# Both attention heads' scores side by side in three PSUM banks, five banks for the rest, and the row sums transposed first in a round

## The chip, the cores and the metric

The kernel runs on one core of one Trainium2 chip. The engines are named as the profile names them: PE (TensorE, the matrix multiplier, with PEld for its weight loads), DVE (VectorE), ACT (ScalarE), POOL (GpSimd) and SP (SyncE, which issues the transfers). PE writes its results to PSUM, a memory of eight banks of 512 fp32 values in each of 128 partitions; DVE and ACT read them there. The metric is the device time of one execution in microseconds (us), as the median of several runs.

## The reference, cut to what matters

Two transformer layers over 512 latent tokens and 256 context tokens (768 in all), 1024 features, everything in fp32. Layer 0 mixes tokens with grouped-query attention (16 query heads, 4 key heads), layer 1 with latent attention (16 heads). Latent queries attend to all 768 keys; in layer 0 the context queries attend to the 256 context keys.

```python
def block_attention(q, k, v):
    def one_block(qi):                                   # 128 queries
        s = jnp.einsum('bqhgd,bkhd->bhgqk', qi, k) * scale
        p = jax.nn.softmax(s, axis=-1)
        return jnp.einsum('bhgqk,bkhe->bqhge', p, v)
...
for i in range(DEPTH):                                   # 2 layers
    y_lat, y_ctx = gqa_mixer(...) if i == 0 else mla_mixer(...)
    x = layer_norm(alpha * x + g_a * y_lat, ...)
    x = layer_norm(alpha * x + g_m * sq_relu_mlp(x * (1 + sc_m) + sh_m, w1, w2), ...)
    # layer 0 does the same for the context tokens
```

## The kernel before

The program runs through its stages once: the modulation vectors and layer 0's projections (to about 129 us), the first attention (to about 340 us), its output projection, layer 0's MLP, layer 1's projections, the second attention (1074 to about 1265 us), its output projection and layer 1's MLP. The products run as fp32r matmuls on operands that are split into a high and a low part (names ending in h and l, or H and L).

Both attentions are `Attn.run` (L752), with 8 pairs of heads. The work is cut into rounds. A full round is one block of 128 queries for both heads of a pair; there are four per pair in each attention, 64 in all. The first attention has one more round per pair for the 256 context queries, 8 in all. The order of PE's instructions within the attentions is that of the code (`manual_schedule`, L785); the order on the other engines is set by a scheduler. In each pass of the loop PE does, in this order:

1. the scores of this round, first head, then second head (`score`, L766, with L848 in layer 0, L840 for context queries, L1351 in layer 1). A head's 768 scores per query lie in a tile `big` of two banks, 384 in each. There are two such tiles, one per head and round, so a tile comes back in the next round.
2. the transposes of the round before (`turn`, L776): 12 per full round (L707), into three tiles `one` of one bank each, which ACT (L710) and DVE (L712) copy to SBUF as `pT`.
3. the end of a finished product with the values, where there is one (`end`, L736): two transposes of the reciprocal row sums (L740) into the bank that holds the product, a copy by ACT (L742) and a multiply by DVE (L743).
4. a preparation step of the next pair, where there is one (L800): transposes of queries (L610, L1307) or a key projection (L89 to L91), through a `one`.
5. half of the product of an earlier pair of rounds with the values (L731), into a `one` that stays taken until its `end`.

Behind each head's scores, DVE finds the row maximum (L690, result `nm`) and ACT the exponentials and their sums (L691, an ACTIVATE followed by a read of the accumulator, result `prob`). In a context round these are L693 and two activations of L695. There are four tiles `one`; two `big` tiles of two banks and four `one` make up the eight banks. During the first attention POOL and the DMA queues work on modulation vectors of later stages, and PE, ACT and DVE have small instructions of that work and of the query preparation among those of the rounds.

A tile that is to be overwritten makes the writer wait until the readers of what is in it have finished. The wait stands in the program as a count of finished instructions on the reader's engine.

Of the kernel before, what the change touches and what calls it, by code (L numbers as in the profile page):

```python
# [11 lines left out]
F32 = mybir.dt.float32  # L12
F32R = mybir.dt.float32r
AF = mybir.ActivationFunctionType
# [25 lines left out]
def backbone(ctx, tc, a, out):  # L40
# [9 lines left out]
    const = pool(ctx, "const")  # L50
    wpool = pool(ctx, "wpool")
    dram = pool(ctx, "dram", space=DRAM)
    ps = pool(ctx, "ps", space=PSUM)

    def big():
        return ps.tile([P, 2, 512], F32, name="big", tag="big", bufs=2)

    def one():
        return ps.tile([P, 512], F32, name="one", tag="one", bufs=4)

    def split_hi(dst, src):
        return nc.scalar.copy(out=dst, in_=src)  # L62
# [610 lines left out]
    class Attn:  # L673
# [6 lines left out]

        def softmax(self, S, ntile, width, sm):


            ap = self.ap
            nm = ap.tile([P, 2], F32, name="nm", tag="nm", bufs=3)
            pt = ap.tile([P, 768], F32, name="prob", tag="prob", bufs=4)
            pv = pt[:, 0 : 2 * width].rearrange("p (b w) -> p b w", b=2)
            sv = S[:, :, 0:width]
            if ntile == 1:
                nc.vector.tensor_reduce(out=nm[:, 0:1], in_=sv, axis=AX.XY, op=ALU.max, negate=True)  # L690
                nc.scalar.activation(pv, sv, AF.Exp, bias=nm[:, 0:1], accum_out=sm)  # L691
            else:
                nc.vector.tensor_reduce(out=nm, in_=sv, axis=AX.X, op=ALU.max, negate=True)  # L693
                for i in range(2):
                    nc.scalar.activation(  # L695
                        pv[:, i], sv[:, i], AF.Exp, bias=nm[:, i : i + 1], accum_out=sm[:, i : i + 1]
                    )
            return pt
# [53 lines left out]
        def run(self, first, prep, scores, vcol, o_of, npair, ctx_scores, fill, at):  # L752

            rounds = []
            for p in range(npair):
                rounds += [(p, 0, 0)] + ([(p, None, 0)] if ctx_scores is not None else [])  # L760
                rounds += [(p, 0, 1), (p, 1, 0), (p, 1, 1)]
            state, PT, sums = {0: first}, {}, {}
            av, steps, ends, last = [], [], [], []
            n = 0

            def score(p, hf, q, h):  # L766
                S = big()
                if (p, hf) not in sums:
                    sums[p, hf] = self.ap.tile([P, 2, 2], F32, name="sm", tag="sm", bufs=4)
                if hf is None:  # L770
                    ctx_scores(state[p], h, S)
                    return self.softmax(S, 2, CTX, sums[p, hf][:, :, h])
                scores(state[p], h, NCT + hf * 2 + q, S)
                return self.softmax(S, 1, 384, sums[p, hf][:, q, h : h + 1])

            def turn(p, hf, q, pts):  # L776
                if hf is None:
                    PT[p, hf] = t = self.ap.tile([P, 2, NCT, 2, P], F32, name="pC", tag="pC")
                    self.transposed(pts, t.rearrange("p t n h c -> p (t n) h c"), 1)
                    return  # L780
                if q == 0:
                    PT[p, hf] = self.ap.tile([P, 2, NT, 2, P], F32, name="pT", tag="pT", bufs=2)
                self.transposed(pts, PT[p, hf][:, q], self.nact)

            with tc.manual_schedule(engines={nc.tensor.engine}):  # L785
                while rounds or last or av or ends:
                    now = []
                    if rounds:
                        p, hf, q = rounds.pop(0)
                        if hf == 0 and q == 0 and p + 1 < npair:  # L790
                            state[p + 1], steps = prep(p + 1)
                        now = [(p, hf, q, [score(p, hf, q, h) for h in range(2)])]
                    ready, ended = av[:1], ends
                    ends = []
                    for it in last:
                        turn(*it)
                    for f in ended:
                        f()
                    if steps:
                        steps.pop(0)()  # L800
                    for f, end in ready:
                        f()
                        ends += [end] if end else []
                    av = av[1:]
                    if last and (last[0][1] is None or last[0][2] == 1):
                        p, hf = last[0][:2]
                        lo = 0 if hf is None else NCT + hf * 2
                        av += self.values(
                            PT[p, hf], sums[p, hf],
                            lambda kt, hh, p=p: vcol(kt, 2 * p + hh), range(NCT if hf is None else NT),  # L810
                            o_of(p)[:, lo : lo + 2, :],
                        )
                    last = now
                    for i in (n, n + 1):
                        if fill is not None:
                            fill(i % 5 < 2)
                        for f in at.get(i, []):
                            f()
                    n += 2
                if fill is not None:  # L820
                    fill.rest()

    st_x.close()
    st_att = ExitStack()
# [15 lines left out]
    def ctx_scores0(st, h, S):  # L840
        pr, QS = st
        kv = pr // 2
        for i in range(2):
            lhsT = QS[h][:, i * P : (i + 1) * P]
            nc.tensor.matmul(S[:, i, 0:CTX], lhsT, KL[:, kv, 0:CTX], start=True, stop=False)
            nc.tensor.matmul(S[:, i, 0:CTX], lhsT, KH[:, kv, 0:CTX], start=False, stop=True)

    def scores0(st, h, qt, S):  # L848
        pr, QS = st
        kv = pr // 2  # L850
        lhsT = QS[h][:, qt * P : (qt + 1) * P]
        for c in range(2):
            cs = slice(c * 384, c * 384 + 384)
            nc.tensor.matmul(S[:, c, 0:384], lhsT, KL[:, kv, cs], start=True, stop=False)
            nc.tensor.matmul(S[:, c, 0:384], lhsT, KH[:, kv, cs], start=False, stop=True)

    phase[0] = "pool"
    ada_ts, ada_bias4 = [], vec_bias(0, 4, 0, 1)
# [492 lines left out]
    def scores1(st, h, qt, S):  # L1351
        kh, kl, QH, QL = st
        cols = slice((qt - NCT) * P, (qt - NCT + 1) * P)
        for c in range(2):
            cs = slice(c * 384, c * 384 + 384)
            nc.tensor.matmul(S[:, c, 0:384], QL[:, h, cols], kh[:, h, cs], start=True, stop=False)
        for c in range(2):
            cs = slice(c * 384, c * 384 + 384)
            nc.tensor.matmul(S[:, c, 0:384], QH[:, h, cols], kl[:, h, cs], start=False, stop=False)
            nc.tensor.matmul(S[:, c, 0:384], QH[:, h, cols], kh[:, h, cs], start=False, stop=True)  # L1360

    o1 = {}

# [141 lines left out]
```

## Time and profile before

| | |
|---|---|
| median of 3 runs | 1697.6 us (1696.79 to 1701.78) |
| the profiled execution's own time | 1703.23 us |
| its span, first to last instruction | 1701.4 us |
| PE busy | 1629.9 us (96% of the span) |
| DVE, ACT, POOL busy | 1111.5, 719.5, 450.6 us |
| mean granted TensorE clock | 0.989 of full speed |

The span is the time from the first to the last recorded instruction; the execution's own time is 1.83 us more. Busy times add up the instructions of an engine; PE's matmuls overlap, so that a row's duration is longer than the step from one matmul to the next. An idle time is named by what ended it. The granted clock is 1.00 at full speed and 0.50 at the lower of TensorE's two levels (2.4 and 1.2 GHz).

### The profile page before, as it was taken

The page shows a single profiled execution, that of the slowest core. Times are in us where ns is not written, and L with a number is a line of the kernel's source. Part 1 is how long each engine was busy: PE and PEld are TensorE (multiplying, and loading weights), DVE is VectorE, ACT ScalarE, POOL GpSimd, SP SyncE. Part 2 cuts the span into 40 slices and gives each one's busy share as a digit, 9 for nine tenths or more (in the row PEclk, how much of TensorE's full clock was granted, in tenths as well). Part 3 has the DMA queues.
Part 4 walks back from the last instruction along what each step waited for, and adds up shares of the span by engine and source line. Part 5 has one row for each costly group of instructions (what it writes and reads, how often), then busy time and mean ns, then how long its engine had stood idle before and what let it go on. Part 6 is the DMA issues. An engine that isn't in the chain of part 4 may idle for free.

```text
span 1701.4 us, 23714 instructions
## 1 busy us (share of the span) xinstructions
PE 1629.9 (96%) x9266; PEld 1369.1 (80%) x9266; DVE 1111.5 (65%) x1700; ACT 719.5 (42%) x1317; POOL 450.6 (26%) x317
## 2 busy tenths in 40 slices
PE   8997998999999999999999899999999999999996
PEld 6775776778888888898889798888778888888884
DVE  4778778755756666556447776766658655555577
ACT  3324666644633344333122356666663532222221
POOL 0247889000323345224003431000004200000034
PEclk9998999999999999999999999999999999999998
DMA  8312113033434356344212232001013533322322
GB/s 323 133 66 90 51 57 100 26 136 112 161 122 138 112 184 198 114 147 146 68 50 85 73 104 90 1 1 38 21 60 122 182 99 99 99 98 88 99 75 75
DMA packets 51969, 172.05 MB, mean 101 GB/s; under 512 B 6776, under 2 KB 6928, under 8 KB 51856
## 3 DMA queue, kind: packets, MB, share of 16 engines
q1 hardware_dynamic: 51824, 170.51, 29.8%
q8 instruction: 73, 1.20, 0.3%
q14 instruction: 40, 0.33, 0.1%
q10 hardware_dynamic: 32, 0.02, 0.0%
HBM read 161.03 MB, written 9.47 MB: 100 GB/s over the span
## 4 chain that ended last, share of the span: by engine, by line
PE 68%; DVE 12%; DMA 7%; POOL 6%; ACT 4%; issue 2%; SPq 0%; DVEq 0%; POOLq 0%; ACTq 0%
PE one L89 9%; PE one L91 9%; PE one L90 9%; PE big L977 7%; PE big L981 6%; PE big L980 6%; DMA araw<-in_w_ada_dram 4%; PE one L731 4%; PE one L917 2%; PE one L921 2%; PE one L918 2%; DVE wl L65 2%; PE one L707 2%; POOL aacc L208 2%; DMA raw<-in_mlp_w_dram 2%
## 5 line engine op out<-in xcount | busy, mean ns | idle before, releaser
L62 ACT CAST wh<-raw 128x1024 fp32r<-128x1024 f32 (+3 forms) x172 | 171.9, 1016 | 399.3 <-PE one L91 213.2
L65 DVE TENSOR_TENSOR wl<-raw,wh 128x1024 fp32r<-128x1024 f32 (+3 forms) x172 | 219.8, 1291 | 173.1 <-ACT wh L62 171.6
L977 PE MATMUL big<-actH,wh 128*128 128x384 f32 (+2 forms) x800 | 280.4, 351 | 1.6 <-ACT wh L62 1.6
L981 PE MATMUL big<-actH,wl 128*128 128x384 f32 (+2 forms) x800 | 279.7, 350 | 0.8 <-DVE wl L65 0.8
L980 PE MATMUL big<-actL,wh 128*128 128x384 f32 (+2 forms) x800 | 279.6, 350 | 0.0
L89 PE MATMUL one<-wh,hh 128*128 128x512 f32 x640 | 256.3, 402 | 12.6 <-ACT hh L62 7.0
L91 PE MATMUL one<-wh,hl 128*128 128x512 f32 x640 | 254.5, 399 | 5.3 <-DVE hl L65 5.3
L90 PE MATMUL one<-wl,hh 128*128 128x512 f32 x640 | 255.5, 399 | 1.3 <-DVE wl L65 1.3
L1059 DVE TENSOR_TENSOR yacc<-yacc,one 128x512 f32<-128x512 f32 x260 | 174.0, 682 | 109.9 <-PE one L91 109.6
L208 POOL TENSOR_TENSOR xr<-xr,raw 128x1024 f32<-128x1024 f32 x49 | 129.7, 2647 | 244.8 <-ACT raw L206 229.6
L977 PEld LDWEIGHTS big<-actH,wh 128*128 128x128 f32 x800 | 150.1, 188 | 15.0 <-ACT wh L62 2.4
L981 PEld LDWEIGHTS big<-actH,wl 128*128 128x128 f32 x800 | 150.1, 188 | 14.1 <-DVE wl L65 1.4
L980 PEld LDWEIGHTS big<-actL,wh 128*128 128x128 f32 x800 | 150.2, 188 | 12.3 <-issue 0.4
L89 PEld LDWEIGHTS one<-wh,hh 128*128 128x128 f32 x640 | 122.0, 191 | 44.5 <-ACT hh L62 8.0
L691 ACT ACTIVATE prob<-big,nm 128x768 f32<-128x768 f32 x128 | 116.2, 908 | 92.2 <-DVE nm L690 91.8
L91 PEld LDWEIGHTS one<-wh,hl 128*128 128x128 f32 x640 | 121.5, 190 | 35.0 <-DVE hl L65 6.2
L90 PEld LDWEIGHTS one<-wl,hh 128*128 128x128 f32 x640 | 122.1, 191 | 27.5 <-DVE wl L65 1.7
L328 POOL TENSOR_TENSOR xr<-xr,ln_g 128x1024 f32<-128x1024 f32 x14 | 37.2, 2658 | 390.9 <-DMA xr<-xres 384.6
L690 DVE TENSOR_REDUCE nm<-big 128x1 f32<-128x768 f32 x128 | 119.8, 954 | 31.8 <-PE big L1360 19.0
L707 PE MATMUL one<-ident,prob 128*128 128x128 f32 x832 | 104.8, 275 | 2.9 <-ACT pT L710 2.0
L731 PE MATMUL one<-pT,V 128*64 128x256 f32 x768 | 98.0, 391 | 5.7 <-DVE pT L712 4.5
L707 PEld LDWEIGHTS one<-ident,prob 128*128 128x128 f32 x832 | 96.0, 142 | 6.8 <-ACT pT L710 2.7
(245 smaller groups left out, 2822.9 us busy)
## 6 DMA issues: line engine op xcount, KB each, us to landing
raw<-in_mlp_w_dram SPq DMA_DIRECT2D x128, 512.0 KB
raw<-in_w_ada_dram SPq DMA_DIRECT2D x56, 512.0 KB
sraw<-in_w_ada_dram SPq DMA_DIRECT2D x16, 512.0 KB
araw<-in_w_ada_dram SPq DMA_DIRECT2D x32, 256.0 KB
raw<-in_w_o_dram SPq DMA_DIRECT2D x16, 512.0 KB
xr<-xres SPq DMA_DIRECT2D x14, 512.0 KB
raw<-in_w_qkv_dram SPq DMA_DIRECT2D x12, 512.0 KB
xres<-z SPq DMA_DIRECT2D x10, 512.0 KB
```

The lines of the kernel that those rows point to most:

```text
L62: return nc.scalar.copy(out=dst, in_=src)
L65: return nc.vector.tensor_tensor(out=dst, in0=src, in1=hi.bitcast(F32), op=ALU.subtract)
L89: nc.tensor.matmul(o, lh, rh, start=start, stop=False)
L90: nc.tensor.matmul(o, lh, rl, start=False, stop=False)
L91: nc.tensor.matmul(o, ll, rh, start=False, stop=stop)
L208: nc.gpsimd.tensor_tensor(out=accs[s], in0=accs[s], in1=dst, op=ALU.add)
L707: nc.tensor.transpose(tp[:, j * P : (j + 1) * P], pts[j % 2][:, k * P : (k + 1) * P], ident)
L731: nc.tensor.matmul(acc[64 * hh : 64 * hh + 64, 0:256], v(kts[n], hh), PT[:, :, n, hh, :], start=(n == 0), stop=(n == len(kts) - 1),)
L977: mm = nc.tensor.matmul(o, wh[:, ks], aH[:, k, s:e], start=(k == 0), stop=False)
L980: nc.tensor.matmul(o, wh[:, ks], aL[:, k, s:e], start=False, stop=False)
L981: nc.tensor.matmul(o, wl[:, ks], aH[:, k, s:e], start=False, stop=(k == KD - 1))
L1059: nc.vector.tensor_tensor(out=yacc[i][:, cs], in0=yacc[i][:, cs], in1=accs[hf], op=ALU.add)
```

## The change

The two `big` tiles of the attentions are gone. While an attention runs, PSUM is laid out anew: one tile `scores` of three banks, in which the first head takes the columns 0 to 767 and the second head 768 to 1535, and five tiles `one` instead of four. The first head's scores fill bank 0 and half of bank 1, the second head's the other half of bank 1 and bank 2, and the matmuls are cut at the bank borders: 512 and 256 columns for the first head, 256 and 512 for the second, in place of 384 and 384. After the attention the layout of before is set up again. In a round, `end` is called before `turn`.

```diff
+    def psum_layout(nbig):
+        if psum:
+            psum["st"].close()
+        psum["st"] = ExitStack()
+        psum["p"] = pool(psum["st"], f"ps{nbig}", space=PSUM)
+        psum["n"] = 8 - 2 * nbig if nbig else 5
 
     def big():
-        return ps.tile([P, 2, 512], F32, name="big", tag="big", bufs=2)
+        return psum["p"].tile([P, 2, 512], F32, name="big", tag="big", bufs=2)
 
     def one():
-        return ps.tile([P, 512], F32, name="one", tag="one", bufs=4)
+        return psum["p"].tile([P, 512], F32, name="one", tag="one", bufs=psum["n"])
+
+    psum_layout(2)
...
             if ntile == 1:
-                nc.vector.tensor_reduce(out=nm[:, 0:1], in_=sv, axis=AX.XY, op=ALU.max, negate=True)
-                nc.scalar.activation(pv, sv, AF.Exp, bias=nm[:, 0:1], accum_out=sm)
+                nc.vector.tensor_reduce(out=nm[:, 0:1], in_=S, axis=AX.X, op=ALU.max, negate=True)
+                nc.scalar.activation(pt, S, AF.Exp, bias=nm[:, 0:1], accum_out=sm)
...
+            psum_layout(0)
+            both = psum["p"].tile([P, 2 * NTOK], F32, name="scores")
             rounds = []
...
             def score(p, hf, q, h):
-                S = big()
+                S = both[:, h * NTOK : (h + 1) * NTOK]
...
                     ready, ended = av[:1], ends
                     ends = []
+                    for f in ended:
+                        f()
                     for it in last:
                         turn(*it)
-                    for f in ended:
-                        f()
...
+            psum_layout(2)
+
+    cuts = ((slice(0, 512), slice(512, NTOK)), (slice(0, 256), slice(256, NTOK)))
...
     def ctx_scores0(st, h, S):
         for i in range(2):
             lhsT = QS[h][:, i * P : (i + 1) * P]
-            nc.tensor.matmul(S[:, i, 0:CTX], lhsT, KL[:, kv, 0:CTX], start=True, stop=False)
-            nc.tensor.matmul(S[:, i, 0:CTX], lhsT, KH[:, kv, 0:CTX], start=False, stop=True)
+            cs = slice(i * CTX, i * CTX + CTX)
+            nc.tensor.matmul(S[:, cs], lhsT, KL[:, kv, 0:CTX], start=True, stop=False)
+            nc.tensor.matmul(S[:, cs], lhsT, KH[:, kv, 0:CTX], start=False, stop=True)
...
-        for c in range(2):
-            cs = slice(c * 384, c * 384 + 384)
-            nc.tensor.matmul(S[:, c, 0:384], lhsT, KL[:, kv, cs], start=True, stop=False)
-            nc.tensor.matmul(S[:, c, 0:384], lhsT, KH[:, kv, cs], start=False, stop=True)
+        for cs in cuts[h]:
+            nc.tensor.matmul(S[:, cs], lhsT, KL[:, kv, cs], start=True, stop=False)
+            nc.tensor.matmul(S[:, cs], lhsT, KH[:, kv, cs], start=False, stop=True)
```

`scores1` of layer 1 is changed in the same way as `scores0`. Outside the two attentions the order on PE is the same; on DVE, ACT and POOL it differs at a few places.

Below is the order on PE in a round of the second attention, before. `KPH` and `KPL` are the high and low parts of the keys, `QH` and `QL` those of the queries; a wait is named by the engine that is waited for. The first six matmuls (in five rows) are the first head's scores, the next six the second head's.

```order
L1356 MATMUL big<-KPH_9427,QL 128x384 x2
L1359 MATMUL big<-KPL_9428,QH 128x384
L1360 MATMUL big<-KPH_9427,QH 128x384
L1359 MATMUL big<-KPL_9428,QH 128x384
L1360 MATMUL big<-KPH_9427,QH 128x384
L1356 MATMUL big<-KPH_9427,QL 128x384 [waits Activation_49]
L1356 MATMUL big<-KPH_9427,QL 128x384
L1359 MATMUL big<-KPL_9428,QH 128x384
L1360 MATMUL big<-KPH_9427,QH 128x384
L1359 MATMUL big<-KPL_9428,QH 128x384
L1360 MATMUL big<-KPH_9427,QH 128x384
```

The same place in the changed program, where L1373, L1375 and L1376 are the three lines of the scores:

```order
L1373 MATMUL scores<-KPH_9356,QL 128x512 [waits Activation_49]
L1373 MATMUL scores<-KPH_9356,QL 128x256
L1375 MATMUL scores<-KPL_9357,QH 128x512
L1376 MATMUL scores<-KPH_9356,QH 128x512
L1375 MATMUL scores<-KPL_9357,QH 128x256
L1376 MATMUL scores<-KPH_9356,QH 128x256
L1373 MATMUL scores<-KPH_9356,QL 128x256 [waits Activation_49]
L1373 MATMUL scores<-KPH_9356,QL 128x512
L1375 MATMUL scores<-KPL_9357,QH 128x256
L1376 MATMUL scores<-KPH_9356,QH 128x256
L1375 MATMUL scores<-KPL_9357,QH 128x512
L1376 MATMUL scores<-KPH_9356,QH 128x512
```

The second head's first matmul waits for ACT in both. By the count that it waits for, this is before the exponential of the second head's tile in the round ahead (on banks 2 and 3), and in the changed program the exponential of the first head in the same round (on banks 0 and 1), whose scores are the rows just above. All 64 full rounds have this wait. In the 8 context rounds the second head waits likewise for the first head's second activation, although the first head's scores lie in bank 0 alone and the second head's in banks 1 and 2 (the tile is one). The first head's first matmul waits for the second head's exponential of the round ahead.

The second place is the first attention, a context round and what follows its scores, before (`rb` are the reciprocal row sums, `q` the queries of a later pair):

```order
L845 MATMUL big<-KL,QS 128x256 [waits Activation_49]
L846 MATMUL big<-KH,QS 128x256
L845 MATMUL big<-KL,QS 128x256
L846 MATMUL big<-KH,QS 128x256
L707 MATMUL one<-ident,prob 128x128 x4
L707 MATMUL one<-ident,prob 128x128 [waits DVE_49]
L707 MATMUL one<-ident,prob 128x128 x3
L707 MATMUL one<-ident,prob 128x128 [waits DVE_49,PE_49]
L707 MATMUL one<-ident,prob 128x128 x3
L740 MATMUL one<-ident,rb 128x128 x2
L610 MATMUL one<-ident,q_1224 128x128 [waits Activation_49]
```

And in the changed program, where L864 and L865 are the lines of the context scores, L752 and L719 those of the sums and of the probabilities, and L622 that of the queries:

```order
L864 MATMUL scores<-KL,QS 128x256 [waits DVE_49,Activation_49]
L865 MATMUL scores<-KH,QS 128x256
L864 MATMUL scores<-KL,QS 128x256
L865 MATMUL scores<-KH,QS 128x256
L752 MATMUL one<-ident,rb 128x128 x2
L719 MATMUL one<-ident,prob 128x128 [waits PE_49]
L719 MATMUL one<-ident,prob 128x128 x3
L719 MATMUL one<-ident,prob 128x128 [waits PE_49]
L719 MATMUL one<-ident,prob 128x128 x3
L719 MATMUL one<-ident,prob 128x128 [waits PE_49]
L719 MATMUL one<-ident,prob 128x128 x3
L622 MATMUL one<-ident,q_1224 128x128 [waits DVE_49,PE_49]
```

The two transposes of the sums have moved ahead of the twelve of the probabilities, and the second head's scores have a wait for DVE and ACT where they waited for ACT.

## Rows read from the trace of the kernel before

**Rows 1.** The page's first part: busy time and share of the span by engine.

```profile
PE 1629.9 (96%) x9266; PEld 1369.1 (80%) x9266; DVE 1111.5 (65%) x1700; ACT 719.5 (42%) x1317; POOL 450.6 (26%) x317
```

**Rows 2.** Windows: length; busy PE, PEld, DVE, ACT, POOL; clock; DMA share; GB/s.

```profile
130.00:333.00 203.00, 181.15 (x1370) 141.43 (x1369) 160.24 (x261) 127.59 (x310) 144.15 (x124) 0.97 0.19 64
130.00:170.00 40.00, 29.34 (x211) 21.52 (x210) 32.08 (x57) 17.82 (x42) 29.15 (x25) 0.87 0.22 77
1074.00:1265.00 191.00, 188.32 (x1296) 154.80 (x1296) 124.02 (x180) 126.15 (x274) 0.00 (x0) 1.00 0.05 18
```

**Rows 3.** Timeline (start us, duration us, instruction [idle before <-releaser]): second attention, one softmax.

```profile
1149.77 0.33 PE L1360 MATMUL big<-KPH,QH 128*128 128x384 f32 x1
1149.94 0.51 PE L1356 MATMUL big<-KPH,QL 128*128 128x384 f32 x2
...
1150.14 0.96 DVE L690 TENSOR_REDUCE nm<-big 128x1 f32<-128x768 f32 x1 [0.53 <-PE big L1360]
...
1151.13 0.90 ACT L691 ACTIVATE prob<-big,nm 128x768 f32<-128x768 f32 x1 [1.04 <-DVE nm L690]
1151.94 0.19 ACT L691 ACTIVATION_READ_ACCUMULATOR prob<-big,nm 128x1 f32 x1
```

**Rows 4.** Timeline: first attention, two matmuls behind the two longest idle times.

```profile
146.80 0.19 ACT L691 ACTIVATION_READ_ACCUMULATOR prob<-big,nm 128x1 f32 x1
...
147.04 0.69 PE L854 MATMUL big<-KL,QS 128*128 128x384 f32 x1 [3.25 <-ACT prob L691]
...
166.15 0.55 PE L610 MATMUL one<-ident,q 128*128 128x128 f32 x3 [2.47 <-ACT pT L710]
```

**Rows 5.** Timeline: first attention, a context round's softmax.

```profile
134.51 0.68 DVE L693 TENSOR_REDUCE nm<-big 128x2 f32<-128x512 f32 x1
...
136.05 0.20 ACT L695 ACTIVATION_READ_ACCUMULATOR prob<-big,nm 128x1 f32 x1
```

**Rows 6.** Timeline of PE: the round with the least work behind its scores.

```profile
199.23 0.34 PE L855 MATMUL big<-KH,QS 128*128 128x384 f32 x1
...
201.82 0.45 PE L854 MATMUL big<-KL,QS 128*128 128x384 f32 x1
```

**Rows 7.** Waits of PE in the first attention (us in total, times, longest us).

```profile
PE one L731 <- DVE pT L712: 6.5, 13, 1.7
```

**Rows 8.** Lines of DVE in the first attention (busy us, mean ns | idle before).

```profile
L690 DVE TENSOR_REDUCE nm<-big 128x1 f32<-128x768 f32 x64 | 58.7, 952 | 10.9 <-PE big L855 10.3
L712 DVE COPY pT<-one 128x512 f32<-128x512 f32 x62 | 39.9, 680 | 1.9 <-PE one L707 1.7
...
L693 DVE TENSOR_REDUCE nm<-big 128x2 f32<-128x512 f32 x16 | 10.4, 685 | 1.6 <-PE big L846 1.4
```

**Rows 9.** Windows of 2.5 us in the first attention, columns as in rows 2.

```profile
145.00:147.50 2.50, 0.46 (x1) 0.46 (x2) 2.44 (x5) 1.50 (x3) 2.50 (x3) 0.77 0.00 0
...
152.50:155.00 2.50, 2.50 (x26) 1.25 (x26) 0.75 (x2) 0.00 (x0) 2.50 (x3) 0.87 0.02 7
165.00:167.50 2.50, 1.35 (x9) 0.87 (x11) 1.92 (x4) 2.34 (x6) 2.28 (x3) 0.86 0.00 0
...
170.00:172.50 2.50, 2.50 (x24) 2.50 (x22) 1.98 (x4) 1.13 (x4) 2.11 (x2) 0.95 0.00 0
```

**Rows 10.** Timeline of PE: first matmul after five idle times outside the attentions.

```profile
457.93 0.50 PE L89 MATMUL one<-wh,hh 128*128 128x512 f32 x1 [2.06 <-ACT yacc L1057]
...
530.48 0.50 PE L89 MATMUL one<-wh,hh 128*128 128x512 f32 x1 [2.81 <-DVE yacc L1059]
...
943.19 0.50 PE L89 MATMUL one<-wh,hh 128*128 128x512 f32 x1 [2.25 <-ACT hh L62]
...
946.50 0.79 PE L91 MATMUL one<-wh,hl 128*128 128x512 f32 x1 [2.57 <-DVE hl L65]
...
1347.83 0.79 PE L91 MATMUL one<-wh,hl 128*128 128x512 f32 x1 [2.78 <-DVE hl L65]
```

More of the change, by code (lines that the diff above doesn't have):

```diff
@@ L52, in backbone @@
     dram = pool(ctx, "dram", space=DRAM)
-    ps = pool(ctx, "ps", space=PSUM)
+    psum = {}
+    def psum_layout(nbig):
[4 more added lines that the diff above has]
+        psum["n"] = 8 - 2 * nbig if nbig else 5
     def big():
-        return ps.tile([P, 2, 512], F32, name="big", tag="big", bufs=2)
+        return psum["p"].tile([P, 2, 512], F32, name="big", tag="big", bufs=2)
     def one():
-        return ps.tile([P, 512], F32, name="one", tag="one", bufs=4)
+        return psum["p"].tile([P, 512], F32, name="one", tag="one", bufs=psum["n"])
+    psum_layout(2)
+    ctx.callback(lambda: psum["st"].close())
     def split_hi(dst, src):
@@ L686, in softmax @@
             pt = ap.tile([P, 768], F32, name="prob", tag="prob", bufs=4)
-            pv = pt[:, 0 : 2 * width].rearrange("p (b w) -> p b w", b=2)
-            sv = S[:, :, 0:width]
             if ntile == 1:
-                nc.vector.tensor_reduce(out=nm[:, 0:1], in_=sv, axis=AX.XY, op=ALU.max, negate=True)
-                nc.scalar.activation(pv, sv, AF.Exp, bias=nm[:, 0:1], accum_out=sm)
-            else:
+                nc.vector.tensor_reduce(out=nm[:, 0:1], in_=S, axis=AX.X, op=ALU.max, negate=True)
+                nc.scalar.activation(pt, S, AF.Exp, bias=nm[:, 0:1], accum_out=sm)
+            else:
+                pv = pt[:, 0 : 2 * width].rearrange("p (b w) -> p b w", b=2)
+                sv = S[:, 0 : 2 * width].rearrange("p (b w) -> p b w", b=2)
                 nc.vector.tensor_reduce(out=nm, in_=sv, axis=AX.X, op=ALU.max, negate=True)
@@ L1353, in scores1 @@
         cols = slice((qt - NCT) * P, (qt - NCT + 1) * P)
[L1354 to L1360, printed above, removed]
+        for cs in cuts[h]:
+            nc.tensor.matmul(S[:, cs], QL[:, h, cols], kh[:, h, cs], start=True, stop=False)
+        for cs in cuts[h]:
+            nc.tensor.matmul(S[:, cs], QH[:, h, cols], kl[:, h, cs], start=False, stop=False)
+            nc.tensor.matmul(S[:, cs], QH[:, h, cols], kh[:, h, cs], start=False, stop=True)
     o1 = {}
```

## The prediction

> **What bounds the kernel now.** Start with the page's first part: PE is busy for 1629.9 of 1701.4 us [rows 1], so time can be lost or won where PE stands still. Then cut the span into stages and read the two that the change touches. In the first attention (130 to 333 us) PE is busy for 181.2 of 203 us, in the second (1074 to 1265 us) for 188.3 of 191 us [rows 2]. So PE is idle for 21.8 us in the one and 2.7 us in the other: 24.5 us is all that better buffering in PSUM can give back. No other engine is near its limit over a whole attention (DVE has 160.2 and 124.0 us). Of the idle time, the list of waits puts most, 6.5 us in 13 times, on value products that wait for DVE's copies out of `one` [rows 7]; a fifth bank goes to such waits.
>
> Next, read one softmax in the order of time, to see what runs beside it [rows 3]. The first head's last score matmul starts at 1149.77, the second head's first one at 1149.94, 0.17 us behind. The first head's row maximum starts on DVE at 1150.14, its exponential on ACT at 1151.13, and the read of the accumulator ends at 1152.13 (1151.94 + 0.19). All of it lies beside PE's work: the second head's scores, then transposes. This cover is what the change touches.
>
> **The change part by part.** *The second head's scores now wait for the first head's exponential.* In the changed program the second head's first score matmul waits for the exponential of the scores that PE has only just written; before, it waited for one a round older. PE takes its matmuls in order, so transposes, preparation steps and value products stand behind the waiting matmul, and nothing covers the softmax of the first head. From the start of the last score matmul to the end of the accumulator's read are 2.36 us (1149.77 to 1152.13) [rows 3]. A score matmul that an exponential released started 0.05 us after such a read (146.80 + 0.19 = 146.99, then 147.04) [rows 4]. So the second head starts 2.41 us after the first head's last matmul where it started 0.17 us after it: 2.24 us more per full round. 64 rounds: 143 us.
>
> In a context round the first head has a maximum of 0.68 us and two activations. From the start of its maximum to the end of the last read are 1.74 us (134.51 to 136.25) [rows 5]; with the 0.37 us ahead of it (1149.77 to 1150.14 in rows 3) and 0.05 us behind it that makes 2.16 us, less the 0.17 us from one matmul to the next: 1.99 us. 8 rounds: 16 us.
>
> *A rule that speaks against the change.* Rows of before can't tell whether the wait is needed, since no bank held two heads. The Trainium skill (PSUM — Partial Sum Buffer, "PSUM bank collisions raise a hardware error") says that two engines must not access one bank in the same quadrant at the same time. By that rule the wait can't be dropped in the full rounds, where half of bank 1 is each head's, and this speaks against the change itself. In the context rounds the heads share no bank; by the rule alone the sum would be 16 us less, but the program has the wait there too. No run so far shows it.
>
> *The other direction.* The first head's first matmul waits for the second head's exponential of the round ahead. The shortest stretch between the second head's last score matmul and the next round's scores is 2.59 us (199.23 to 201.82) [rows 6], against the 2.41 us that the softmax takes. It stays hidden, by little; I put 0 for it, with 0.3 us in 8 rounds as the most.
>
> *Buffers and the order in a round.* The fifth bank and the earlier transposes of the sums, whose bank is then free sooner, act on waits as in rows 7. These mostly go in any case: while PE stands, DVE and ACT catch up with their copies. Of the 24.5 us idle I take two thirds as recovered, 16 us: nearly half of the first attention's 21.8 us lies before 170 us (40 - 29.3 = 10.7) [rows 2], where DVE is late and a stall costs the less. The bounds are 0 and 24.5.
>
> *Where the chain meets other work.* DVE and ACT may be busy when the first head's scores are done. Beside the maxima (58.7 and 10.4 us) DVE does 91 us in the 40 rounds of the first attention [rows 2, 8], 2.3 us in each, of about 7.3 us that a round will take. So a maximum meets a running instruction in about 3 of 10 rounds and waits for half of it, 0.34 us for the copies of 680 ns [rows 8]: 0.1 us a round, 7 us in 72. From no collision to nearly every round, 0 to 20 us.
>
> *Matmul shapes, the new layout.* 512 + 256 columns are as many as 384 + 384, and as many matmuls: 0. Setting up the layout twice puts a few waits for old tiles at each border, where PE would wait for the same scores' inputs: 0, at most 2 us.
>
> *The clock.* Idle time can lower PE's clock. In the first attention the granted clock fell twice, to 0.50: at the end of 3.25 us of idle time (145 to 155 us) and just behind 2.47 us (165 to 172.5 us) [rows 4, 9]. From the shares in rows 9 it was low for about 6.8 and 3.4 us; in that time PE did half of the work, so 3.4 and 1.7 us were lost. Outside the attentions, three idle times of 2.06, 2.81 and 2.25 us left the clock as it was (the next 512-column matmul takes 0.50 us), and two of 2.57 and 2.78 us did not (0.79 us) [rows 10]. So of six such gaps between 2 and 3 us three lowered it. The new gaps of 2.24 us are at the lower end of these, but there are 72, each about 5 us after the last. I take one in three, 24, at 2.1 us each (nearer to the shorter of the two low stretches): 50 us. The bounds are 0, and 72 times 1.7 us = 122 us.
>
> The Trainium skill (TensorE: Matmul & The Clock Gate, "Why this matters for your kernels") ties a drop of the clock to gaps longer than these. The gap of 2.47 us [rows 4] speaks against the rule, that of 2.81 us [rows 10] for it; what it gives is the first rival below.
>
> **The sum**, against the profiled execution's own 1703.2 us: + 143 + 16 - 16 + 7 + 50 = + 200 us, which gives 1903 us. That execution is 5.6 us above the median of the runs, 1697.6 us; from the median it is 1898 us. The low end: 1697.6 + 159 - 24.5 = 1832 us, with no loss by the clock. The high end: 1697.6 + 159 + 20 + 122 = 1999 us, nothing recovered and every gap lowering the clock.
>
> **The rivals.**
> 1. *The stalls come, the clock holds.* For it: three of six gaps left the clock alone. Against it: 2.47 us lowered it in this very stage, and the new gaps return every 7 to 8 us. 1697.6 + 143 + 16 - 16 + 7 = 1848 us.
> 2. *The clock falls at nearly every stall.* For it: no gap in the rows comes back so soon as these. Against it: gaps of 2.06 and 2.25 us that did nothing. 1848 + 122 = 1970 us.
> 3. *Not slower: the softmax of the first head is over before PE needs it, or the wait is in truth for the round ahead.* Then the fifth bank and the earlier sums take away the waits of rows 7 and as much again of the other idle time, some 12 us: 1686 us. It decides from the point where the second head's first matmul starts within 0.2 us of the first head's last; against it stand 2.36 us from rows 3 and the count behind the wait.
>
> **How the numbers follow.** The forecast of 1898 us has a chance of 0.53 (1865 to 1940 us is its own range), rival 1 0.29, rival 2 0.13, rival 3 0.05. The range from 1830 to 1970 us takes in rival 1 and half of rival 2. A measurement of this kernel can tell 0.3%, about 5 us, from no change. All cases but rival 3 are slower by far more: slower 0.95; rival 3's 0.05 is split into faster 0.03 and same 0.02, since 12 us are little more than that bound.
>
> **What would show it.** In the profile after: the waits of PE headed by the score lines for the exponential, about 72 times and 2.2 us each; the second head's first score matmul some 2.4 us behind the first head's last; the windows of both attentions longer by 60 to 110 us each with PE's busy share near 70%; few waits left for DVE's copies; the granted clock below 1.00 in windows of both attentions. The rest of the span stays as it is, within a few us. I am wrong if the second head's scores follow the first head's at once, or if the stages outside the attentions carry the difference.

## The result, and the profile after

The changed kernel takes 1917.4 us (median of 4 runs, 1907.37 to 1920.79), the kernel before 1697.8 us beside it: 1.1275 times as long, interval 1.1246 to 1.1303. The forecast was 1898 us, the range 1830 to 1970 us. The profiled execution is the shortest of the four: 1907.37 us, a span of 1905.6 us, 204.2 us longer than before.

First the page's part 1, which answers to [rows 1], and the rows for PE and its clock of part 2 (40 slices of the span, in tenths).

```profile
PE 1688.0 (89%) x9266; PEld 1400.5 (73%) x9266; DVE 1118.5 (59%) x1700; ACT 729.4 (38%) x1317; POOL 447.0 (23%) x317
...
PE   8977676679999999999998998777778989999996
...
PEclk9987999899999999999999998888888999999998
```

The same 9266 matmuls keep PE busy for 58.1 us longer (1688.0 against 1629.9). The other engines do what they did, within 10 us each. But for the last slice, which is as before, PE's busy share and its clock are lowest in the slices of the two attentions.

Next the waits of PE, which answer to [rows 7] (us in total, times, longest us).

```profile
PE scores L872 <- ACT prob L701: 82.0, 32, 13.0
PE scores L1373 <- ACT prob L701: 69.5, 34, 2.5
PE scores L864 <- ACT prob L707: 15.3, 8, 2.2
```

These are 167 us; before, score matmuls waited 5.2 us for exponentials. L872 and L1373 are the full rounds of the two attentions, L864 the context rounds. No wait of PE for a copy of `pT` that the list counts is left.

Then the stages, each from its first score matmul to its last: before, and after (columns as in [rows 2]).

```profile
128.84:329.05 200.21, 178.65 (x1346) 139.83 (x1345) 158.11 (x259) 125.16 (x304) 145.31 (x125) 0.97 0.20 67
1074.40:1259.85 185.45, 182.77 (x1249) 150.52 (x1249) 120.81 (x174) 121.64 (x264) 0.00 (x0) 1.00 0.05 18
```

```profile
128.57:423.34 294.77, 196.87 (x1345) 144.66 (x1346) 161.50 (x258) 131.24 (x306) 143.21 (x125) 0.92 0.13 45
1168.50:1463.25 294.75, 225.22 (x1247) 179.16 (x1248) 119.76 (x169) 126.67 (x261) 0.00 (x0) 0.85 0.03 11
```

Subtract PE's busy time from the length. PE's idle time went from 21.6 to 97.9 us in the first attention and from 2.7 to 69.5 us in the second, + 143.2 us together. Its busy time went up by 18.2 and 42.5 us, together 60.7 us, as the granted clock fell from 0.97 to 0.92 and from 1.00 to 0.85. 143.2 + 60.7 = 203.9 us is the longer span but for 0.3 us, so the stages outside the attentions carry no part of it.

One full round in the order of time, in the second attention, answers to [rows 3].

```profile
1252.28 0.28 PE L1376 MATMUL scores<-KPH,QH 128*128 128x256 f32 x1
1252.60 0.96 DVE L700 TENSOR_REDUCE nm<-scores 128x1 f32<-128x768 f32 x1 [0.53 <-PE scores L1376]
1253.59 0.90 ACT L701 ACTIVATE prob<-scores,nm 128x768 f32<-128x768 f32 x1 [2.12 <-DVE nm L700]
1254.39 0.19 ACT L701 ACTIVATION_READ_ACCUMULATOR prob<-scores,nm 128x1 f32 x1
1254.64 0.97 PE L1373 MATMUL scores<-KPH,QL 128*128 128x256 f32 x2 [2.08 <-ACT prob L701]
...
1255.84 0.63 PE L1375 MATMUL scores<-KPL,QH 128*128 128x512 f32 x1
```

Read it downwards: the first head's last matmul, its maximum, its exponential, the read of the accumulator, and 0.06 us behind the read's end the second head's first matmul. From the first head's last matmul to it are 2.36 us, where [rows 3] have 0.17. The 512-column matmul behind the stall takes 0.63 us; at the full clock it takes 0.40 (the same one a round earlier, at 1246.87). The duration of the maximum and the exponential hasn't changed.

### The profile page after: what moved, and what is told of

The parts are those of the page before. It is cut to its first block, busy times and chain, and to the rows that moved or that the text cites. A ratio compares the mean times of both kernels' runs of the same rounds, so it can differ in the third digit from the quotient of the medians.

```text
span 1905.6 us, 23712 instructions
## 1 busy us (share of the span) xinstructions
PE 1688.0 (89%) x9266; PEld 1400.5 (73%) x9266; DVE 1118.5 (59%) x1700; ACT 729.4 (38%) x1317; POOL 447.0 (23%) x317
## 4 chain that ended last, share of the span: by engine, by line
PE 73%; DVE 13%; ACT 7%; DMA 3%; POOL 2%; issue 2%; DVEq 0%; SPq 0%; ACTq 0%; POOLq 0%
PE one L101 8%; PE one L103 8%; PE one L102 8%; PE big L995 6%; PE big L999 6%; PE big L998 6%; PE one L719 6%; PE one L743 5%; ACT prob L701 4%; DVE nm L700 3%; PE one L935 2%; PE scores L1373 2%; DVE wl L77 2%; PE one L939 2%; PE one L936 2%; PE scores L872 2%
## 5 line engine op out<-in xcount | busy, mean ns | idle before, releaser
L700 DVE TENSOR_REDUCE nm<-scores 128x1 f32<-128x768 f32 x128 | 122.5, 957 | 209.7 <-PE scores L1376 115.3
L701 ACT ACTIVATE prob<-scores,nm 128x768 f32<-128x768 f32 x128 | 115.5, 902 | 160.5 <-DVE nm L700 160.1
L999 PEld LDWEIGHTS big<-actH,wl 128*128 128x128 f32 x800 | 150.1, 188 | 13.5 <-DVE wl L77 1.0
L719 PE MATMUL one<-ident,prob 128*128 128x128 f32 x832 | 133.2, 323 | 0.0
L719 PEld LDWEIGHTS one<-ident,prob 128*128 128x128 f32 x832 | 124.3, 172 | 7.1 <-issue 2.6
L872 PE MATMUL scores<-KL,QS 128*128 128x512 f32 (+1 forms) x128 | 50.4, 404 | 82.1 <-ACT prob L701 82.0
```

Of the source, the lines that this page charges most:

```text
L700: nc.vector.tensor_reduce(out=nm[:, 0:1], in_=S, axis=AX.X, op=ALU.max, negate=True)
L701: nc.scalar.activation(pt, S, AF.Exp, bias=nm[:, 0:1], accum_out=sm)
L719: nc.tensor.transpose(tp[:, j * P : (j + 1) * P], pts[j % 2][:, k * P : (k + 1) * P], ident)
L999: nc.tensor.matmul(o, wl[:, ks], aH[:, k, s:e], start=False, stop=(k == KD - 1))
```

## The experiments

Every kernel ran beside the kernel before on the same chip, and each ratio is against it.

### Two tiles of two banks

```diff
-        psum["n"] = 8 - 2 * nbig if nbig else 5
+        psum["n"] = 8 - 2 * nbig if nbig else 4
-            both = psum["p"].tile([P, 2 * NTOK], F32, name="scores")
+            both = [psum["p"].tile([P, 2 * 512], F32, name=f"scores{h}") for h in range(2)]
-                S = both[:, h * NTOK : (h + 1) * NTOK]
+                S = both[h][:, 0:NTOK]
-    cuts = (..., (slice(0, 256), slice(256, NTOK)))
+    cuts = (..., (slice(0, 512), slice(512, NTOK)))
```

> The changed kernel with the two heads' scores in two tiles of two banks each (512 and 256 columns), and four tiles one; the sums are still transposed first. Theory A (the shared tile's wait is the whole cause, 141 us of stalls in full rounds, 15 in context rounds, and the lower clock that follows from them): the waits of the score lines for the exponential vanish, the clock is back at 0.99, and the time is that of before within 10 us, 1688 to 1703 us; with the earlier sums it may be up to 8 us below. Rival B (the new order of the sums or the 512 + 256 cut costs a good part): over 1750 us.

Measured: 1710.3 us, ratio 1.0061 (1.0039 to 1.0082). The stalls are gone (the one wait of a score line above 2 us is one of 4.3 us in the first rounds), and of 12.75% more time 0.6% is left. That is 7 us past the range of theory A, and rival B is far off; later experiments come back to the 0.6%.

### One tile, each head with banks of its own

```diff
-            both = psum["p"].tile([P, 2 * NTOK], F32, name="scores")
+            both = psum["p"].tile([P, 4 * 512], F32, name="scores")
-                S = both[:, h * NTOK : (h + 1) * NTOK]
+                S = both[:, h * 1024 : h * 1024 + NTOK]
```

The rest is as in the run with two tiles: the same banks, cuts and order.

> One tile of four banks instead of two tiles of two: each head has banks 0 and 1 or banks 2 and 3 to itself, both within the same tile, all else as in the run with two tiles (1710 us). Theory A (the wait belongs to the tile: a head's matmuls wait for the last reader of the tile, whatever its banks): the stalls come back whole, 64 of about 2.1 us and 8 of about 1.9 us in the context rounds, and 1905 to 1925 us. Rival B (the wait belongs to the bank that both heads share, so banks of their own are enough): 1705 to 1715 us, the context rounds' stalls alone at most 20 us more. In between would mean that the wait is kept for some of the rounds.

Measured: 1911.3 us, ratio 1.1258 (1.1235 to 1.1281). Its waits of PE:

```profile
PE scores L872 <- ACT prob L701: 80.9, 33, 13.0
PE scores L1373 <- ACT prob L701: 69.3, 34, 3.0
PE scores L864 <- ACT prob L707: 15.6, 8, 2.2
```

The heads share no bank, and the stalls are all there. So in this program the wait belongs to the tile: the second head's matmuls wait for the reader of the first head's part, though it lies in other banks. Theory A held, rival B fell.

### The sums last again

```diff
-                    for f in ended:
-                        f()
                     for it in last:
                         turn(*it)
+                    for f in ended:
+                        f()
```

> The changed kernel with only the order in a round set back: the transposes of the probabilities first, then those of the sums. Theory A: the stalls are set by the shared tile, so 1905 to 1930 us, the same as the change within 1%. Rival B (the order is a part of the loss): 1860 us or less. Rival C (the earlier sums give back much of the idle time of before): 1935 us or more.

Measured: 1906.1 us, ratio 1.1212 (1.1179 to 1.1245), and the score waits are as in the changed kernel (79.5, 68.0 and 15.8 us). So the order in a round makes up at most 0.6% of the 12.75%, and not the stalls. Theory A held.

### The stall filled with matmuls

Eight matmuls of 512 columns, whose result nobody reads, stand ahead of the second head's scores and take a `one` for it. Nothing else is left out or changed.

```diff
             def score(p, hf, q, h):
+                if h == 1:
+                    idle = one()
+                    t = ...                         # the pair's queries
+                    for _ in range(8):
+                        nc.tensor.matmul(idle, t[:, 0:P], t[:, 0:512], start=True, stop=True)
```

> The changed kernel with eight matmuls of 512 columns that nothing reads put into each wait, ahead of the second head's scores (about 1.9 us of the 2.24 us). Theory A (of the 220 us, about 59 are PE's work at the lower clock, caused by the idle time): the granted clock goes to 0.98 or more, the waits shrink to about 0.3 us, PE's other rows last as long as before, and the time falls to 1850 to 1875 us. Rival (the score matmuls and transposes are slower for another reason, as their banks or shapes): the clock may rise, but the time stays at 1905 us or more.

Measured: 1854.0 us, ratio 1.0904 (1.0874 to 1.0933), a mean clock of 0.990. The attentions:

```profile
129.45:407.54 278.09, 256.54 (x1665) 188.48 (x1666) 160.42 (x258) 131.56 (x306) 143.80 (x125) 0.98 0.15 48
1151.40:1409.19 257.79, 244.47 (x1504) 187.45 (x1505) 119.58 (x169) 125.43 (x261) 0.00 (x0) 1.00 0.04 13
```

With more work for PE the kernel is 63 us faster than the changed one, and the granted clock is 0.98 and 1.00 where it was 0.92 and 0.85. The second head's scores start as late as without the filling, so that these 63 us come from the clock and not from the waiting itself. Between the two profiled executions (1853.76 and 1907.37 us) it is 53.6 us. Theory A held.

### Other work between the heads

The sums and the transposes of the round before are placed between the two heads' scores; the shared tile stays.

```diff
-                        now = [(p, hf, q, [score(p, hf, q, h) for h in range(2)])]
+                        now = [(p, hf, q, [score(p, hf, q, 0)])]
...
                     for it in last:
                         turn(*it)
+                    for p, hf, q, pts in now:
+                        pts.append(score(p, hf, q, 1))
```

> The changed kernel with the sums and the transposes of the round before put between the first and the second head's scores. Theory A: 1.3 to 1.5 us of PE work cover as much of each 2.24 us stall; what is left there is 0.7 to 0.9 us a round, and the second head's own softmax is now covered only by the preparation step and the value products (1.5 to 2.6 us), which adds 0 to 0.9 us in front of the next round: 72 rounds of about 1 us, with the clock above 0.98: 1740 to 1800 us. Rival (the engines behind, not the order on PE, set the pace of the rounds): 1860 us or more.

Measured: 1811.6 us, ratio 1.0652 (1.0621 to 1.0684), a miss of 12 us past the range's end. The clock holds (0.984), but the waits for exponentials and for what they release still sum to some 115 us. One part of the reason is in the order of time:

```profile
1241.03 1.47 PE L719 MATMUL one<-ident,prob 128*128 128x128 f32 x12
1241.22 0.96 DVE L700 TENSOR_REDUCE nm<-scores 128x1 f32<-128x768 f32 x1 [0.32 <-PE scores L1378]
1241.66 1.07 ACT L722 COPY pT<-one 128x512 f32<-128x512 f32 x2 [1.35 <-PE one L719]
...
1242.62 0.92 ACT L701 ACTIVATE prob<-scores,nm 128x768 f32<-128x768 f32 x1
1243.42 0.21 ACT L701 ACTIVATION_READ_ACCUMULATOR prob<-scores,nm 128x1 f32 x1
1243.68 0.61 PE L1375 MATMUL scores<-KPH,QL 128*128 128x256 f32 x2 [1.19 <-ACT prob L701]
```

The maximum ends at 1242.18, but ACT's two copies of transposes last to 1242.73, and the exponential stands behind them in ACT's queue: it starts at 1242.62 (as the second copy ends; the rows overlap by 0.11 us), nearly half a microsecond late. In this round the transposes that cover PE make the copies that hold up the exponential. And now the first head's scores wait too (54 and 52 waits where there were 32 and 34), since less work lies between the second head's and the next round's scores.

### The shared tile in the second attention alone

The first attention as in the run with two tiles, the second as in the changed kernel.

> The shared three-bank tile in the second attention alone; the first attention has a tile of two banks for each head. Theory A (the stalls make up the loss of each attention by itself): the second attention is longer by 109 us as in the changed kernel, the first by less than 10 us, and the total is 1800 to 1825 us. Rival B (the clock's loss is carried over from the first attention into the second): the second attention is longer by 70 us or less with a granted clock above 0.95, and the total is 1770 to 1780 us.

Measured: 1814.0 us, ratio 1.0667 (1.0650 to 1.0685). The two attentions:

```profile
129.63:327.38 197.75, 177.27 (x1346) 134.02 (x1345) 158.99 (x259) 123.52 (x304) 145.10 (x125) 0.97 0.21 69
1074.88:1369.52 294.64, 225.18 (x1247) 179.19 (x1248) 119.66 (x169) 126.44 (x261) 0.00 (x0) 0.85 0.04 11
```

The second row agrees with that of the changed kernel to 0.1 us (294.64 and 294.75 us, busy 225.18 and 225.22 us): each attention loses for itself, and nothing is carried from the first into the second.

### What the 0.6% of the two tiles is

Two tiles with the sums last (the edit of "The sums last again" on top of the two tiles), and the kernel before with the sums first (the same edit in the other direction, alone).

> Two tiles of two banks as before in this study, with the sums transposed last in a round as in the kernel before; the cut of 512 and 256 columns stays. Theory A (the 0.6% of the two tiles is the order, since a preparation step that takes a bank follows straight behind the transposes whose bank ACT still reads): 1695 to 1703 us, the same as before. Rival B (it is the cut of 512 and 256 columns, or the fixed tiles): 1707 to 1713 us.

> The kernel before with one edit: the sums are transposed first in a round. Theory A (the order costs 0.6%): 1705 to 1713 us, ratio 1.004 to 1.009. Rival B (the order costs nothing, the cut or the fixed tiles do): 1695 to 1702 us.

Measured: 1705.0 us, ratio 1.0027 (1.0014 to 1.0041), and 1700.7 us, ratio 0.9997 (0.9987 to 1.0008). Neither theory explains both: the order gives back a half of it with two tiles and costs nothing in the kernel before. The stages of the latter show two effects that cancel:

```profile
129.05:320.31 191.26, 177.35 (x1346) 138.19 (x1345) 156.34 (x259) 123.75 (x304) 143.54 (x125) 0.98 0.22 71
1067.51:1258.61 191.10, 183.27 (x1249) 150.35 (x1249) 120.02 (x174) 120.78 (x264) 0.00 (x0) 1.00 0.05 18
```

Against before, the first attention is 9 us shorter and the second 6 us longer. In the first, the waits of value products for DVE's copies [rows 7] fall from 13 to one. In the second, the preparation steps now follow straight behind the transposes and wait for the bank that ACT still copies: L89 and L1307 wait for `pT` 19 times, 4.5 us, where it was 9 times, 1.8 us; two score matmuls wait 2.3 us for queries that come later. The two tiles with the sums first have the second effect without the first. Their second attention:

```profile
1075.99:1267.40 191.41, 183.69 (x1248) 143.76 (x1249) 119.12 (x169) 120.34 (x259) 0.00 (x0) 1.00 0.05 17
```

It is 6 us longer than before, with the same waits for `pT` (4.3 us) and for queries (2.2 us); their first attention, 200.81 us, is not shorter, and in it PE waits once for 5.6 us for DVE's query work, where it was 0.9 us. So the order accounts for 6 us of the 0.6%, as far as these executions show. With the sums last, the attentions of the two tiles are 200.73 and 185.57 us, together 0.6 us longer than before: the fixed tiles and the 512 and 256 cut cost next to nothing there. The 0.27% left, 5 us by the medians, lies in the profiled executions for the most part outside the attentions and stays open.

### Other work between the heads, with a tile for each

The placement between the heads, first with two fixed tiles, then as one edit in the kernel before, with the sums last and with the sums first.

> Two tiles of two banks, one per head, and the transposes of the round before placed between the two heads' scores. Theory A (the shared tile is the loss; with a tile per head nothing waits for an exponential of the same round): no score wait above 1 us in sum outside the first round, and 1700 to 1715 us, since the transposes now follow the exponential sooner and their copies on ACT stand ahead of the next exponential. Rival B (the placement between the heads is itself good once nothing waits): 1690 to 1700 us, better than the kernel before. Rival C (ACT's copies ahead of the exponential cost 1 us in a round even with two tiles): about 1770 us.

> The kernel before with one edit: the transposes of the round before and the transposed sums stand between the two heads' scores. Theory A (the placement is worth what it gave with two tiles, where it took 1710 to 1694 us with the sums first, since each head's scores then find the other work between them and the tile of two banks free): 1685 to 1697 us, ratio 0.990 to 0.998. Rival B (with two rotating tiles nothing was left to gain: 24.5 us of idle time in the attentions of before, most of it ahead of 170 us where DVE is late): 1697 to 1703 us.

> As the run with the placement between the heads in the kernel before, and the sums first as in the changed kernel. Theory A (the order of the sums decides nothing by itself): within 3 us of that run. Rival B (the sums first are what made the placement good with two tiles): 4 us or more faster than that run.

Measured: 1693.9 us, ratio 0.9970 (0.9957 to 0.9984); 1691.7 us, ratio 0.9938 (0.9919 to 0.9956); and 1689.9 us, ratio 0.9922 (0.9902 to 0.9942). The first lies within rival B's range: with a tile for each head the placement gains 0.9% on its own base (1.0061 to 0.9970), where with the shared tile it gained more, 1.1275 to 1.0652, and was still 6.5% slower than before. Theory A held in the other two. The last has the lowest median of the study. Its attentions, and a piece of the second:

```profile
128.65:323.36 194.71, 181.17 (x1360) 138.42 (x1360) 160.38 (x262) 132.71 (x309) 145.42 (x125) 0.97 0.22 70
1067.89:1248.50 180.61, 179.35 (x1263) 151.19 (x1264) 121.63 (x176) 127.58 (x269) 0.00 (x0) 1.00 0.06 19
```

```profile
1147.33 1.47 PE L707 MATMUL one<-ident,prob 128*128 128x128 f32 x12
1147.53 0.96 DVE L690 TENSOR_REDUCE nm<-big 128x1 f32<-128x768 f32 x1 [0.18 <-PE big L1362]
1147.96 1.07 ACT L710 COPY pT<-one 128x512 f32<-128x512 f32 x2 [1.21 <-PE one L707]
1148.56 0.60 PE L1358 MATMUL big<-KPH,QL 128*128 128x384 f32 x2
...
1148.92 0.92 ACT L691 ACTIVATE prob<-big,nm 128x768 f32<-128x768 f32 x1
```

The copies stand ahead of the exponential here as well, but the second head's scores start at 1148.56, before the exponential does. The second head's scores also stand between the transposes and the preparation step, so that ACT has time to empty the bank: the waits of L89 and L1307 for `pT`, 19 with the sums first alone, are gone. PE's idle time in the second attention falls from 2.7 to 1.3 us, in the first from 21.6 to 13.5 us, which the sums first alone had brought to 13.9. Busy time in the second falls by 3.4 us and rises in the first by 2.5 us; why is open.

## Why the prediction was right

The likeliest case came true, and its mechanism, a softmax that nothing covers in every round, can be found in the profile step by step. Two of the smaller terms, the first head's waits and the clock, came out near for reasons that were not the ones given, and a third, the collisions, has another shape. By its own terms, for the profiled execution:

| term | predicted | measured | where it is seen |
|---|---|---|---|
| second head waits, 64 full rounds | +143 | +138.5 | the waits L872 and L1373, less the next two rows' parts in them |
| first head waits for the round ahead | 0, at most 2.4 | +2.2 | two of the 34 waits of L1373 (1.45 and 0.74 us) |
| collisions on DVE and ACT | +7 | +10.8 | the 13.0 us wait of L872, less a usual 2.2 |
| context rounds | +16 | +15.3 | the wait L864 |
| idle time recovered | -16 | -23.6 | 24.2 us before; 167.4 - 166.8 us after |
| lower clock | +50 | +60.7 | PE's busy time, of which about 54 are the clock's |
| sum | +200 | +203.9 | |

*The stall.* 138.5 us in 64 rounds are 2.16 us each, for 2.24. The chain in time was read off [rows 3] and came out to 0.05 us.

*The other direction* came out near 0 by luck. The 2.59 us of [rows 6] are not the shortest stretch between the second head's last score matmul and the next round's scores. At the start of the second attention, before, two are shorter; this is the first:

```profile
1076.33 0.34 PE L1360 MATMUL big<-KPH,QH 128*128 128x384 f32 x1
...
1077.70 0.61 PE L1356 MATMUL big<-KPH,QL 128*128 128x384 f32 x2
```

They are 1.37 us and, from 1084.60 on, 1.84 us long, too short for a softmax of 2.41 us. The same two rounds are the ones that wait after the change, for 1.45 and 0.74 us; the eight rounds that the prediction had in mind do not.

*The context rounds.* A context round, which answers to [rows 5]:

```profile
147.40 0.41 PE L865 MATMUL scores<-KH,QS 128*128 128x256 f32 x1
...
147.86 0.69 DVE L705 TENSOR_REDUCE nm<-scores 128x2 f32<-128x512 f32 x1 [0.51 <-PE scores L865]
...
149.40 0.20 ACT L707 ACTIVATION_READ_ACCUMULATOR prob<-scores,nm 128x1 f32 x1
149.66 0.58 PE L864 MATMUL scores<-KL,QS 128*128 128x256 f32 x1 [1.84 <-ACT prob L707]
```

Here the heads have separate banks and PE waits all the same, as the prediction read from the program. With the run of one tile and separate banks this settles what the wait is for. The Trainium skill's rule on banks (PSUM — Partial Sum Buffer, "PSUM bank collisions raise a hardware error") may forbid dropping the wait where bank 1 is shared, but it isn't what makes PE wait in this program; what happens with two engines in one bank at once was not tried.

*The collisions* were mis-shaped rather than mis-sized: not 0.1 us in each round but one of 10.8 us in the first, and five other waits of 2.51 to 3.58 us, which the first row of the table contains; most of the rest are of 2.07 to 2.15 us.

```profile
129.23 0.28 PE L873 MATMUL scores<-KH,QS 128*128 128x256 f32 x1
...
137.33 3.23 DVE L616 TENSOR_TENSOR q<-ra,rb 128x128 f32<-128x128 f32 x4
140.49 0.94 DVE L700 TENSOR_REDUCE nm<-scores 128x1 f32<-128x768 f32 x1
...
142.51 0.58 PE L872 MATMUL scores<-KL,QS 128*128 128x256 f32 x1 [12.99 <-ACT prob L701]
```

DVE does 11 us of query work ahead of the first maximum, and the second head's scores now stand behind that. The scheduler set that order; the prediction counted DVE's work per round and did not look at what stood ahead of the first.

*The recovered idle time.* Nearly all of it came back, where two thirds were taken. It was the stalls that did it, by giving DVE and ACT time, not the fifth bank: with four banks and the same stalls (the run of one tile with separate banks) PE's waits for `pT` are 1.7 us, with five none.

*The clock.* One stall in three was taken to lower the clock, 24 of 72, at 2.1 us each. By the last 512-column score matmul behind the stall (0.39 or 0.40 us at full speed, 0.58 to 0.63 at the lower) it was low in 5 of the 32 full rounds of the first attention and in 19 of the 32 of the second, and behind seven others the granted clock fell within 1.4 us: 31 of 72. PE's busy time rose by 60.7 us, but not all of that is the clock's: the run with filled stalls, in its profiled execution, is 150.5 us longer than before and 53.6 us shorter than the changed kernel. So the clock's own term is about 54 us, an estimate from these two executions, or 1.7 us for each of the 31. More drops at a lower price made nearly the 50 us that were put: in part luck. Where the other 7 us of busy time come from was not settled.

The size of a stall did not decide alone: the three of more than 3 us (12.99, 3.48 and 3.58 us) all had the lower clock with or behind them, but stalls of 2.07 us did it in one round and not in another. The Trainium skill's statement (TensorE: Matmul & The Clock Gate, "Why this matters for your kernels"), which ties a drop to longer gaps and gave rival 1 its 1848 us, does not hold here as a bound; the row at 1254.64 has a gap of 2.08 us and the low clock behind it. The run with filled stalls is that rival made real, the same stalls in time with the clock held: 1854 us, 6 us from its number. A reading behind the odds was off as well: the prediction counts the gap of 2.25 us [rows 10] with those that left the clock as it was, but the granted clock fell 1.9 us behind that gap's end, at 945.06, where PE had been idle again for 1.1 us of the 2.57 us gap. These two can't be told apart, and a fast matmul right behind a gap does not show that the clock holds.

*From the execution to the median.* The three other runs have a mean clock of 0.952 to 0.954, the profiled one 0.959. Half a per cent of 1915 us is 10 us, which is most of the 8 to 13 us by which they are longer. The share of full speed that the clock fell short, times the span, went from 0.011 x 1701 = 19 us to 0.041 x 1906 = 78 us in the profiled execution and to 0.047 x 1918 = 90 us in the others, so that the clock's term is some 10 us larger in the median run. The median is 19 us over the forecast: 4 us are the sum above (203.9 for 200), some 10 us this term, and 5.6 us the step down from the profiled execution of before to its median, on which the forecast was put.

Rival 2 (1970 us) wanted the drop at nearly every stall; it came at 31 of 72. Rival 3 fell with the first row of the waits.

## What to carry to other kernels

In this program a wait follows the tile, not the bytes or the bank: before two producers are packed into one tile to save a bank, ask whether the second must now wait for the first one's reader, and whether PE has other work in its queue ahead of that wait. Here the packed layout freed one bank, worth 1.7 us of waits beside the same stalls, and exposed a 2.4 us softmax 64 times. The price of short stalls is their length plus what the clock loses behind them, here about 54 us on 150. Other work placed in front of the wait helps in either layout, 5.5% with the shared tile and 0.9% with two tiles, but it does not make up for the wait: with the shared tile the kernel stays 6.5% slower than before, in part as that work puts ACT's copies ahead of the exponential that PE waits for.

## What the runs showed of the hardware

Stalls of much the same length, mostly 1.83 to 2.2 us, lowered the clock seldom in the first attention, where there are 40 in 295 us, one per 7.4 us (7 of the 40, granted 0.92), and more often than not in the second, where there are 32, one per 9.2 us (24 of the 32, granted 0.85). More frequent stalls were not the worse ones. About half of the first attention's time at the lower clock, 23.9 us of some 47, lies around the one wait of 13.0 us (granted 0.50 from 131.72 to 155.61). What tells the two stages apart was not settled by any run. The second stage's length repeated to 0.1 us in another kernel, so it is no accident of one execution.
